# Transpositions of a scan, sums ahead of and behind them, and eight tiles of an FFN put in other places: an encoder block on one core

## The chip, the cores and the metric

The kernel runs on one core of a Trainium2 chip. The metric is the device time of one execution in microseconds (us), as the median of several runs. A profiled execution gives the trace from which the rows below are taken. The engines are PE (TensorE: matmuls, and transpositions as matmuls with an identity), PEld (PE's weight loads, which overlap its matmuls), DVE (VectorE), ACT (ScalarE), POOL (GpSimd) and SP (SyncE, which issues DMAs). Each engine runs its own list of instructions in order and waits, at the head of that list, for what other engines have to deliver.

## The reference

One residual block on x of 512 tokens by 1024 columns, in float32:

```python
x = x + 0.5 * swiglu(rms_norm(x, ffn1_norm), ffn1_w1, ffn1_w3, ffn1_w2)
h = rms_norm(x, mix_norm); p = h @ w_in
y_a = rwkv7_mixer(token_shift(p[..., :SHIFT_COLS]), ...) @ rwkv_proj
y_b = fox_mixer(p[..., SHIFT_COLS:SHIFT_COLS + FOX_COLS], ...) @ fox_proj
x = x + (sigmoid(g_a) * y_a + sigmoid(g_b) * y_b) @ w_out
x = x + 0.5 * swiglu(rms_norm(x, ffn2_norm), ffn2_w1, ffn2_w3, ffn2_w2)
out = rms_norm(x, final_norm)
```

`swiglu(h, w1, w3, w2)` is `(silu(h @ w1) * (h @ w3)) @ w2` with 2816 inner columns. The RWKV-7 mixer is a recurrence over the tokens with one 64 x 64 state for each of 8 heads; the forgetting attention (fox) has 8 heads of 64 with a causal mask and a decay from cumulated logarithms.

## The kernel before

**Layout and precision.** x is kept transposed, as eight tiles of 128 columns by 512 tokens (`xT`). A float32 product is made as three matmuls of rounded halves, `hi*hi + hi*lo + lo*hi` (`mm3`, L142): ACT casts a weight tile into `whi` (L133), DVE subtracts it from the raw tile into `wlo` (L134), and the moving operand is split likewise. SP loads the raw weights through four buffers.

**The stages.** The first FFN, the input projection with the preparation of the recurrence, a scan of 16 steps, the projections of the two mixers, `w_out`, the second FFN and the final norm. In an FFN, 22 inner tiles of 128 rows are made one after the other (`h0` to `h21`, each as `hh` and `hl`). Most are made by a seven-product scheme on halves of 256 tokens (class `Seven`), whose sums of weights lie in the tiles `wsum`, `wtwo` and `wone`. Then come the down products `pd`: eight output tiles, each of 22 x 3 = 66 matmuls of 512 columns, accumulated in the order of the inner tiles, so the 31st to the 42nd of the 66 read `h10` to `h13`. The last output tile of the second FFN is made in two halves of 256 columns, so that the final norm of the first half runs beside the products of the second. Behind each of the first seven output tiles of the second FFN stand four transpositions `ot` of the tile before (L1709).

**Where the tiles lie.** In both FFNs `h10` to `h13` use the eight places of the x tiles, in a pool at the right end of SBUF (`place_h`, L711). As the built program places them, these eight tiles of the first FFN start at byte 288 modulo 512 in every partition, and those of the second at byte 480 modulo 512. The weights `whi`, `wlo`, the tiles `wtwo` and `wone` and all other operands of the products named here start at byte 288 modulo 512.

**The scan.** A step c, of 16, does on PE: some products of the remaining input projections (`some`, matmuls `pq` and `pgt`, which fill the time), the transpositions `turned` of the attention weights, the solve `ups`, the attention's logits `lp`, further products, at some steps a head sum `pq2` (L1161, over two halves `shi` and `slo`; the listings show it as pq), the next state `sps`, the output `yps`, the attention's values, and the read `xps` of the next step. DVE multiplies `sps` by the decay (RD, L1504), and the next read needs both halves of that. Steps at which no attention unit stands behind them (before steps 1, 2, 6 and 10) have no values between `yps` and `xps`. Every second step a group of four transpositions (`vp` of the values, `stage_v`, or `bp` of the keys, `stage_b`) prepares two later steps; ACT copies the result into RD. The PSUM tiles `vp`, `bp`, `ups`, `sps`, `yps`, `xps` and the head sums of the later pairs take three banks in turn, so each waits until the third one before it has been read. A head sum's bank is read by ACT's logarithm (`qrn`, L1165).

**What sets the order.** Instructions that go through `keep` stay in the order of the program; for others a scheduler with its own model of times chooses the order on each engine. `issue_after` puts an instruction behind another in that order.

**Behind the scan.** `fox(m)` is one of eight projections `ppj` (L1553), whose result DVE adds to a gate and multiplies (L1583). Between `fox(0)` and `fox(1)` four centrings `yc` (two matmuls each, L1590) work on the halves of the scan's output, which ACT and DVE split (L170, L171).

**The end.** For each half of the tokens, `final` squares the last tile, sums the squares over the partitions for two token blocks (`os`, L1730: `facc` holds the first seven tiles' squares, `sq` the last tile's), transposes the last tile (`ot`), takes the root on ACT (L1733, L1734), scales four pieces of 512 columns (L1738 on ACT, L1740 on DVE) and stores them (L1741).

## Time and profile before

| | us |
|---|---|
| median of 3 runs | 1140.15 |
| the runs | 1140.03 to 1140.36 |
| the profiled execution, its own time | 1140.51 |
| its span, first to last instruction | 1138.8 |
| PE busy | 1127.8 |
| DVE busy | 830.0 |
| ACT busy | 600.9 |

The mean granted clock of TensorE is 0.999 of full speed. In rows of a timeline the first number is the start in us from the span's start, the second the duration in us, then the engine, the line, the operation, `out<-in` by the program's names without buffer numbers, the shape, the count of instructions merged into the row, and in brackets the idle time of the engine before it with what ended it. A row of a group has the count, then busy us and mean ns of one, or ns as minimum/median/maximum. Matmuls are pipelined, so a matmul's duration is longer than the time from its start to the next one's; the latter is what a stream of them costs. The chain of waits is followed back from the last instruction: each of its rows has a start, a length, the engine and the work.

### The profile page before, as it was taken

Reading aid. Unit: us, or ns where it says so; the run is one execution under the profiler, and the core shown is the slowest. Engines: PE = TensorE matmul, PEld = TensorE weight load, DVE = VectorE, ACT = ScalarE, POOL = GpSimd, SP = SyncE. Lnnn points to the kernel's source line nnn. Section 1 sums busy time; section 2 is a strip of 40 time slices with the busy share of each in tenths; the row PEclk is TensorE's granted clock in tenths of the full one; section 3 lists DMA queues with packets and bytes.
Section 4 is the critical chain, followed back from the end, with each engine's and each line's share of the span. In section 5 each row is a group of like instructions: output and inputs, shape, how many; then the busy total and the mean of one; then the engine's idle time right before and its main releaser. Section 6 shows DMA issues by size and latency. Waiting matters only on the chain.

```text
span 1138.8 us, 19344 instructions
## 1 busy us (share of the span) xinstructions
PE 1127.8 (99%) x7674; PEld 988.1 (87%) x7674; DVE 830.0 (73%) x1301; ACT 600.9 (53%) x1004; POOL 106.8 (9%) x174
## 2 busy tenths in 40 slices
PE   9999999999999999999999999999999999999997
PEld 7899999988887888888777777888999999988887
DVE  6889999953246888777766668879999999943233
ACT  6645665532226754355877757536555566532121
POOL 2000000010111111321000011132000000010000
PEclk9999999999999999999999999999999999999999
DMA  8433333353334333345113236544333333363321
GB/s 260 135 93 109 97 112 111 95 181 115 112 103 124 103 104 103 112 142 139 38 38 100 67 113 200 177 142 126 103 97 108 111 94 112 107 192 91 89 78 74
DMA packets 210729, 131.14 MB, mean 115 GB/s; under 512 B 10415, under 2 KB 200943, under 8 KB 210639
## 3 DMA queue, kind: packets, MB, share of 16 engines
q1 hardware_dynamic: 202078, 108.67, 32.8%
q0 software_dynamic: 6320, 20.45, 5.4%
q8 instruction: 60, 0.98, 0.4%
q10 hardware_dynamic: 2240, 0.79, 0.3%
q14 instruction: 31, 0.25, 0.1%
HBM read 115.02 MB, written 14.88 MB: 114 GB/s over the span
## 4 chain that ended last, share of the span: by engine, by line
PE 96%; DVE 2%; ACT 1%; issue 1%; DVEq 0%; ACTq 0%
PE pd L142 21%; PE za L142 19%; PE zc L142 14%; PE pgt L142 8%; PE pk L142 6%; PE pw L142 4%; PE ppj L1553 4%; PE pb L142 3%; PE pa L142 3%; PE pq L142 3%; PE pv L142 2%; PE pl L142 1%; PE f L309 1%; PE gp L1076 1%; PE lp L1333 1%; PE lp L1347 1%
## 5 line engine op out<-in xcount | busy, mean ns | idle before, releaser
L133 ACT CAST whi<-raw 128x1024 fp32r<-128x1024 f32 (+3 forms) x117 | 113.8, 974 | 238.4 <-PE pd L142 153.7
L134 DVE TENSOR_TENSOR wlo<-raw,whi 128x1024 fp32r<-128x1024 f32 (+3 forms) x117 | 131.9, 1128 | 120.6 <-ACT whi L133 120.3
L142 PE MATMUL pd<-hh,wlo 128*128 128x512 f32 (+1 forms) x332 | 126.5, 381 | 0.0
L142 PE MATMUL pd<-hh,whi 128*128 128x512 f32 (+1 forms) x332 | 126.1, 380 | 0.0
L142 PE MATMUL pd<-hl,whi 128*128 128x512 f32 (+1 forms) x332 | 126.0, 379 | 0.0
L142 PE MATMUL zc<-xh,whi 128*128 128x256 f32 x296 | 83.8, 283 | 0.0
L142 PE MATMUL zc<-xl,whi 128*128 128x256 f32 x296 | 83.8, 283 | 0.0
L142 PE MATMUL zc<-xh,wlo 128*128 128x256 f32 x296 | 83.8, 283 | 0.0
L142 PEld LDWEIGHTS pd<-hl,whi 128*128 128x128 f32 x332 | 62.4, 188 | 12.0
L142 PEld LDWEIGHTS pd<-hh,whi 128*128 128x128 f32 x332 | 62.4, 188 | 11.7
L142 PEld LDWEIGHTS pd<-hh,wlo 128*128 128x128 f32 x332 | 62.4, 188 | 11.6
L142 PEld LDWEIGHTS zc<-xh,whi 128*128 128x128 f32 x296 | 56.8, 192 | 0.0
L142 PEld LDWEIGHTS zc<-xl,whi 128*128 128x128 f32 x296 | 56.8, 192 | 0.0
L142 PEld LDWEIGHTS zc<-xh,wlo 128*128 128x128 f32 x296 | 56.8, 192 | 0.0
L504 ACT CAST wtwo<-wsum 128x1024 fp32r<-128x1024 f32 x37 | 38.8, 1050 | 32.8 <-PE za L142 32.8
L142 PE MATMUL pgt<-xh,whi 128*128 128x512 f32 x128 | 53.0, 414 | 0.0
L507 DVE TENSOR_TENSOR wlo<-raw,whi 128x1024 fp32r<-128x1024 f32 x41 | 50.0, 1219 | 2.7 <-ACT whi L504 2.7
L516 DVE TENSOR_TENSOR wsum<-wsum,raw 128x512 f32<-128x512 f32 x74 | 50.9, 688 | 1.2
L516 DVE TENSOR_TENSOR wsum<-raw 128x512 f32<-128x512 f32 x74 | 50.6, 684 | 0.0
L142 PE MATMUL pgt<-xh,wlo 128*128 128x512 f32 x128 | 50.2, 392 | 0.0
L142 PE MATMUL pgt<-xl,whi 128*128 128x512 f32 x128 | 50.0, 391 | 0.0
L732 POOL DMA_DIRECT2D xP<-xpark x16 | 8.7, 548 | 438.2 <-PE za L142 437.5
(519 smaller groups left out, 3334.0 us busy)
## 6 DMA issues: line engine op xcount, KB each, us to landing
raw<-in_ffn_w_dram SPq DMA_DIRECT2D x118, 512.0 KB
raw<-in_w_in_dram SPq DMA_DIRECT2D x40, 512.0 KB
raw<-in_ffn_w_dram SPq DMA_DIRECT2D x15, 384.0 KB
xP<-xpark POOLq DMA_DIRECT2D x16, 256.0 KB, 4.7
raw<-in_w_out_dram SPq DMA_DIRECT2D x8, 512.0 KB
gsave<-gs SPq DMA_DIRECT2D x9, 256.0 KB
xin<-in_x_dram SPq DMA_DIRECT2D x4, 512.0 KB
xpark<-xT POOLq DMA_DIRECT2D x8, 256.0 KB, 6.3
```

The source lines that it names most:

```text
L133: marks["wide"] = act.copy(hi[:], raw[:])
L134: marks["rest"] = (eng or dve).tensor_tensor(lo[:], raw[:], hi[:].bitcast(F32), op=ALU.subtract)
L142: mm = pe.matmul(ps, w, x_, start=first and n == 0, stop=last and n == 2, skip_group_check=chain)
L309: return keep(pe.matmul(first[w][:], wt, x_[:], start=k == 0 and n == 0, stop=k == KD - 1 and n == 2))
L504: keep(act.copy(dst, src))
L507: keep(dve.tensor_tensor(dst, src, f32(hi), op=ALU.subtract))
L516: keep(dve.tensor_tensor(to, a, b, op=ALU.add))
L732: nc.gpsimd.dma_start(xT[c][:], xpark[c])
L1076: gm = pe.matmul(gps[g][o, c], BK[s, cc], G[p][q][s, cc], start=True, stop=True)
L1333: keep(pe.transpose(s.lps[q][:, k * P:(k + 1) * P], pts[:, q, k * P:(k + 1) * P], ident[:]))
L1347: keep(pe.matmul(av[half(q), j * P:(j + 1) * P], vt[k][:, h * 64:(h + 1) * 64], s.trs[q][:, o:o + P], start=k == 0, stop=k == b))
L1553: keep(pe.matmul(ps[:], a[:, k, :], y[k][b], start=k == 0 and n == 0, stop=k == NP - 1 and n == 2))
```

## The change

**Transpositions of the scan.** A new function `staged(c)` holds the call of `stage_v` or `stage_b`. For steps 1, 2, 6 and 10 it is called at the end of the step before, ahead of the read; for step 4 it is called behind the first group of products of the step; for the others it stays where it was. On PE, at the read before step 2 (yps is the output of step 1, vp the moved transpositions, xps the read, pq the products), before:

```order
L1435 MATMUL xps<-RD_5173,G_3630 32x64
L1435 MATMUL xps<-RD_5173,G_3631 32x64
L1236 MATMUL vp<-ident,V_3792 64x128 x4
L142 MATMUL pq<-xh_3493,whi 128x512
L142 MATMUL pq<-xl_3494,whi 128x512
```

and now:

```order
L1514 MATMUL yps<-G_3630,RD_5172 64x32
L1514 MATMUL yps<-G_3631,RD_5172 64x32
L1236 MATMUL vp<-ident,V_3792 64x128 x4
L1435 MATMUL xps<-RD_5173,G_3624 32x64
L1435 MATMUL xps<-RD_5173,G_3625 32x64
```

The four transpositions, which stood behind the last read, stand ahead of the first one. By the turn of the three banks, `bp` before step 1 now takes the bank of `ups`, `vp` before steps 2 and 6 that of the head sum, and `vp` before step 10 that of `ups`; the reads take that of `sps`. The scheduler also changes the order on ACT here. The logarithm `qrn` of step 1's head sum goes ahead of the last two exponentials instead of between them. On ACT from the copies of `vp` on (qsq and shi are the square and its rounded half for step 2's head sum, tr copies of transposed attention weights, the RD<-ups rows copies of the solve), before:

```order
L1240 COPY RD_5172<-vp 32x4x64 x4
L1155 ACTIVATE qsq<-qk_5077 128x512
L133 CAST whi<-raw 128x1024
L1338 COPY tr<-lp 128x384
L157 CAST shi<-qsq 128x512
L1338 COPY tr<-lp 128x384
L1479 COPY RD_5173<-ups 32x2x64
L1480 COPY RD_5173<-ups 32x2x64
L1479 COPY RD_5173<-ups 32x2x64
L1480 COPY RD_5173<-ups 32x2x64
```

and now:

```order
L1240 COPY RD_5172<-vp 32x4x64 x4
L133 CAST whi<-raw 128x1024
L1155 ACTIVATE qsq<-qk_5077 128x512
L1338 COPY tr<-lp 128x384 x2
L1485 COPY RD_5173<-ups 32x2x64
L1486 COPY RD_5173<-ups 32x2x64
L1485 COPY RD_5173<-ups 32x2x64
L1486 COPY RD_5173<-ups 32x2x64
L157 CAST shi<-qsq 128x512
```

The cast shi moved behind both copies tr and the four copies of the solve, and the square qsq behind the cast of the weights. On DVE the remainder slo of step 2's head sum, which needs shi, goes behind both maxima of the attention instead of between them, and stays ahead of the decay.

**Sums behind the splits.** `fox(m)`'s sum is put behind the last split by `issue_after`. On DVE behind the scan (yklc, yqb and yv are the remainders that the centrings read, G the sum of fox 0, then of fox 1), before:

```order
L171 TENSOR_TENSOR yklc_7094<-V_3792,yklc_7093 128x512
L171 TENSOR_TENSOR yqb_7096<-V_3792,ykb_7095 128x512
L1583 SCALAR_TENSOR_TENSOR G_3624<-G_3624,ppj 128x512
L171 TENSOR_TENSOR yv_7098<-V_3792,yv_7097 128x512
L171 TENSOR_TENSOR yv_7100<-V_3792,yla 128x512
L134 TENSOR_TENSOR wlo<-raw,whi 128x512
```

and now:

```order
L171 TENSOR_TENSOR yklc_7094<-V_3792,yklc_7093 128x512
L171 TENSOR_TENSOR yqb_7096<-V_3792,ykb_7095 128x512
L171 TENSOR_TENSOR yv_7098<-V_3792,yv_7097 128x512
L171 TENSOR_TENSOR yv_7100<-V_3792,yla 128x512
L1594 SCALAR_TENSOR_TENSOR G_3624<-G_3624,ppj 128x512
L134 TENSOR_TENSOR wlo<-raw,whi 128x512
```

The sum of `fox(0)` moved behind the two remainders yv. The scheduler also puts two of ACT's squares of the centrings behind a weight cast instead of around it.

**Places.** A tile `xpad` of 192 bytes is added to the pool of the x tiles, and `fr`, in a pool that lies below it, grows from 176 to 512 bytes. `h10` to `h13` of the second FFN (and the x tiles `xS` before them) move down by 192 bytes, to byte 288 modulo 512. `wsum`, `wtwo`, `wone`, and the final norm's tiles move down by 512 bytes. Nothing else moves.

**The end.** In `final` both `facc` sums go ahead of the transpositions and both `sq` sums behind them, in an order that is kept; the first piece of each half is cut into two of 256 columns, so that five pieces are scaled and stored for four.

```diff
--- before.py
+++ after.py
@@ -168,7 +168,7 @@
 
     def split(dst_hi, dst_lo, src, hi_eng="act"):
         cast = act.copy(dst_hi, src) if hi_eng == "act" else dve.tensor_copy(dst_hi, src)
-        dve.tensor_tensor(dst_lo, src, dst_hi.bitcast(F32), op=ALU.subtract)
+        marks["part"] = dve.tensor_tensor(dst_lo, src, dst_hi.bitcast(F32), op=ALU.subtract)
         return cast
 
 
@@ -1451,6 +1451,10 @@
         def unit(n):
             return units[places.index(n)] if n in places else None
 
+        def staged(c):
+            if c + 2 < NC:
+                (stage_b if c % 2 else stage_v)(c + 2 - c % 2)
+
         parted.extend((0, n, part) for n, part in enumerate(first_parts))
         with tc.issue_after(ahead.ins):
             Xs, taken = read(0)
@@ -1460,11 +1464,13 @@
             u, v = unit(c - 1), unit(c)
             n = some_of[c]
             late_logits = v and c == 12
-            if c + 2 < NC:
-                (stage_b if c % 2 else stage_v)(c + 2 - c % 2)
+            if c not in (1, 2, 4, 6, 10):
+                staged(c)
             with tc.issue_after(taken.ins):
                 flush(100 if c in (1, 12) else 5)
             some(n[0])
+            if c == 4:
+                staged(c)
             if u:
                 u.turned()
             elif c == 0:
@@ -1515,6 +1521,8 @@
                     flush(1.5)
             if u and c + 1 < NC:
                 u.values()
+            if c + 1 in (1, 2, 6, 10):
+                staged(c + 1)
             if c + 1 < NC:
                 Xs, taken = read(c + 1)
             if ends:
@@ -1576,11 +1584,14 @@
             cut = split(*parts[p], vs[p])
         with tc.issue_after(cut.ins):
             logs = act.preload_act_table_set("natural_log_exp_and_others")
+        split_all = marks["part"]
+
         def fox(m):
             g = gslot[m]
             nc.gpsimd.dma_start(g, gsave[KD + m])
             ps = proj(proj_w(m, fox_proj), ybs)
-            dve.scalar_tensor_tensor(g, g, 1.0, ps[:], op0=ALU.add, op1=ALU.mult)
+            with tc.issue_after(split_all.ins):
+                dve.scalar_tensor_tensor(g, g, 1.0, ps[:], op0=ALU.add, op1=ALU.mult)
 
         ycs, sums, roots = [], [], []
 
@@ -1664,6 +1675,7 @@
             late_tanh(m, parted)
         rtp = ctx.enter_context(tc.tile_pool(name="xr2", bufs=1, side="right"))
         xT[:] = [rtp.tile([P, T], F32, name=f"xS{c}", tag=f"xS{c}") for c in range(KD)]
+        rtp.tile([P, 48], F32, name="xpad", tag="xpad")
         for c in range(KD):
             nc.gpsimd.dma_start(xT[c][:], xsave[c])
         ms = []
@@ -1701,7 +1713,7 @@
         fin["O"] = [fp.tile([P, NB, D // 2], F32, name=f"O{i}", tag=f"O{i}") for i in range(2)]
         fin["acc"] = fp.tile([P, T], F32, name="facc", tag="facc")
         fin["sq7"] = fp.tile([P, T], F32, name="sq7", tag="sq7")
-        fin["fr"] = fp.tile([P, 44], F32, name="fr", tag="fr")
+        fin["fr"] = fp.tile([P, P], F32, name="fr", tag="fr")
 
     def tokens(m, b0, nb):
         ps = pr.tile([P, nb, P], F32, tag="b", name="ot")
@@ -1725,20 +1737,24 @@
         hs = slice(b0 * P, (b0 + 2) * P)
         act.activation(fin["sq7"][:, hs], xT[m][:, hs], AF.Square)
         ps = bank("os", pf)
-        for b in (b0, b0 + 1):
-            for t, st in ((fin["acc"], True), (fin["sq7"], False)):
-                pe.matmul(ps[:, b:b + 1], t[:, b * P:(b + 1) * P], ones[:, 0:1], start=st, stop=not st)
+        def add(t, st):
+            for b in (b0, b0 + 1):
+                keep(pe.matmul(ps[:, b:b + 1], t[:, b * P:(b + 1) * P], ones[:, 0:1], start=st and b == b0, stop=not st, skip_group_check=True))
+
+        add(fin["acc"], True)
         tokens(m, b0, 2)
+        add(fin["sq7"], False)
         r = fin["fr"][:, b0:b0 + 2]
         act.activation(r, ps[:, b0:b0 + 2], AF.Ln, bias=epsr[:, 0:1], scale=1.0 / D)
         act.activation(r, r, AF.Exp, scale=-0.5)
-        for b, c, e in ((b0, 0, dve), (b0 + 1, 1, act), (b0, 1, dve), (b0 + 1, 0, dve)):
-            o = fin["O"][c][:, b]
+        w = D // 4
+        for b, c, at, n, e in ((b0, 0, 0, w, dve), (b0 + 1, 1, 0, 2 * w, act), (b0, 0, w, w, dve), (b0, 1, 0, 2 * w, dve), (b0 + 1, 0, 0, 2 * w, dve)):
+            o = fin["O"][c][:, b, at:at + n]
             if e is act:
                 act.activation(o, o, AF.Copy, scale=fin["fr"][:, b:b + 1])
             else:
                 dve.tensor_scalar(o, o, fin["fr"][:, b:b + 1], None, op0=ALU.mult)
-            nc.sync.dma_start(out[0, b * P:(b + 1) * P, c * 512:(c + 1) * 512], o)
+            nc.sync.dma_start(out[0, b * P:(b + 1) * P, c * 512 + at:c * 512 + at + n], o)
 
     ffn(nrm2, ffn2_w1, ffn2_w3, ffn2_w2, almost, final=final,
         seven={"fast": range(2, 22), "from": 1, "to": 22, "sums": (0, 0), "own": 5, "stream": "xS", "places": places, "after": after})
```

## Prediction

> **What bounds the kernel now.** First the busy times of the page, then the waits of PE over the whole span.
>
> ```profile
> PE 1127.8 (99%) x7674; PEld 988.1 (87%) x7674; DVE 830.0 (73%) x1301; ACT 600.9 (53%) x1004; POOL 106.8 (9%) x174
> ```
>
> PE idles 1138.8 - 1127.8 = 11.0 us in all, some of it in the first 16 us, which nothing here touches. A change can save only part of that idle time, or the length of PE's own work. The waits of PE (us in total, times, longest) say how much idle is in reach:
>
> ```profile
> PE xps L1435 <- DVE RD L1504: 1.0, 4, 0.5
> PE ot L1709 <- DVE xP L847: 0.9, 1, 0.9
> PE vp L1236 <- ACT qrn L1165: 0.5, 1, 0.5
> PE yc L1590 <- DVE yv L171: 0.5, 1, 0.5
> ```
>
> Four waits of the scan's reads (xps), one of a transposition (vp), one of the centring (yc), one in the last chain (ot): 2.9 us, and the edits touch each of them.
>
> **1. Transpositions into the waits before steps 1, 2, 6 and 10.** Now they stand behind the read; then, ahead of it, where PE waits for the decay.
>
> ```profile
> 541.34 0.88 DVE L1504 TENSOR_TENSOR RD<-sps,PC 64x256 f32<-64x256 f32 x2
> ...
> 542.27 0.44 PE L1435 MATMUL xps<-RD,G 128*32 128x64 f32 x14 [0.16 <-DVE RD L1504]
> ...
> 543.06 0.48 PE L142 MATMUL pq<-xh,whi 128*128 128x512 f32 x1
> ```
>
> ```profile
> 552.03 0.68 ACT L1165 ACTIVATE qrn<-pq,epsr 128x512 f32<-128x512 f32 x1
> ...
> 552.76 0.47 PE L1435 MATMUL xps<-RD,G 128*32 128x64 f32 x16 [0.51 <-DVE RD L1504]
> ...
> 553.16 0.62 PE L1236 MATMUL vp<-ident,V 128*64 128x128 f32 x4
> ...
> 553.55 0.48 PE L142 MATMUL pq<-xh,whi 128*128 128x512 f32 x1
> ```
>
> ```profile
> 590.63 0.68 ACT L1165 ACTIVATE qrn<-pq,epsr 128x512 f32<-128x512 f32 x1
> ...
> 591.92 0.28 PEld L1435 LDWEIGHTS xps<-RD,G 128*32 128x32 f32 x14 [0.26 <-DVE RD L1504]
> ...
> 592.68 0.48 PE L142 MATMUL pgt<-xh,whi 128*128 128x512 f32 x1
> ```
>
> ```profile
> 629.89 0.44 PE L1435 MATMUL xps<-RD,G 128*32 128x64 f32 x14 [0.16 <-DVE RD L1504]
> ...
> 630.65 0.48 PE L142 MATMUL pgt<-xh,whi 128*128 128x512 f32 x1
> ```
>
> The second half of the decay still ends when it did, and sixteen reads then take 0.40 (552.76 to 553.16), with 0.03 to the next product. So the product starts at 542.70 for 543.06, 553.19 for 553.55, 592.35 for 592.68, 630.32 for 630.65: 0.36 + 0.36 + 0.33 + 0.33 = **1.38 us**. The cover is the wait itself; without it the transpositions cost what they cost now, 0.39 a step (553.16 to 553.55). Queued behind a transposition that waits are the reads, and behind these the step's solve.
>
> It can wait for its PSUM bank. At steps 2 and 6 the bank is the one a head sum leaves, free once ACT's logarithm has read it. At step 2 that ends at 552.03 + 0.68 = 552.71, too late for any gain; but the new order on ACT puts this logarithm before two exponentials, one of 0.47 ahead of it, so it ends about 0.6 sooner. At step 6 it ends at 590.63 + 0.68 = 591.31, which leaves 0.6 to the reads at 591.92 for 0.39 of transpositions. At steps 1 and 10 the bank is long free. I take the full 1.38; at the worst, steps 2 and 6 gain nothing and it is 0.69.
>
> **2. The transposition of step 4, behind a group of products.**
>
> ```profile
> 572.22 0.45 PE L1435 MATMUL xps<-RD,G 128*32 128x64 f32 x16
> ...
> 573.17 0.63 PE L1236 MATMUL vp<-ident,V 128*64 128x128 f32 x4 [0.51 <-ACT qrn L1165]
> ```
>
> Here 0.95 us pass from reads to transposition, where step 2 needs 0.40. The twelve products that go ahead last 2.7 us, so the bank is free when the transposition's turn comes, and the wait goes: **0.5 us**. The copies of its result come later on ACT, behind them those of this step's solve, which the next state needs only after more products; I charge nothing.
>
> **3. What the scan gives back.** ACT's order in step 2 also changes: the cast of the squares (shi) goes behind a copy (tr) and the four of the solved step, and DVE's remainder (slo) waits for it.
>
> ```profile
> 557.34 0.62 ACT L157 CAST shi<-qsq 128x512 fp32r<-128x512 f32 x1
> 557.87 0.48 ACT L1338 COPY tr<-lp 128x384 f32<-128x384 f32 x1
> ...
> 559.50 0.58 ACT L1319 ACTIVATE pts<-lp,mx 128x384 f32<-128x384 f32 x1
> ```
>
> ```profile
> 558.03 0.68 DVE L158 TENSOR_TENSOR slo<-qsq,shi 128x512 fp32r<-128x512 f32 x1
> ```
>
> ```profile
> 560.38 0.40 PE L1161 MATMUL pq<-slo,bonesr 128*128 128x512 f32 x1
> ```
>
> The cast moves back by 559.50 - 557.87 = 1.63, while ACT's queue is about 0.5 ahead by then (0.36 from step 1, some more since step 2's transposition is ready to copy sooner): cast at 558.47 to 559.09, remainder 559.14 to 559.82. PE, 0.72 ahead by then, wants it at 559.66: a new wait of 0.2 us, between 0 and 0.5. The scan nets 1.38 + 0.5 - 0.2 = **1.7 us**.
>
> **4. Remainders ahead of fox 0's sum on DVE.**
>
> ```profile
> 688.25 0.68 DVE L1583 SCALAR_TENSOR_TENSOR G<-G,ppj 128x512 f32<-128x512 f32 x1
> ...
> 688.85 0.68 DVE L171 TENSOR_TENSOR yv<-V,yv 128x512 fp32r<-128x512 f32 x1
> 689.45 0.68 DVE L171 TENSOR_TENSOR yv<-V,yla 128x512 fp32r<-128x512 f32 x1
> 689.58 0.50 PE L1590 MATMUL yc<-yv,center 128*128 128x512 f32 x1 [0.46 <-DVE yv L171]
> ...
> 690.52 0.39 PE L1553 MATMUL ppj<-yh,whi 128*128 128x512 f32 x1
> ```
>
> Each remainder moves up one DVE slot of 0.60. The waiting product starts near 688.98, and the last one, which needs the second remainder (688.85 + 0.68 = 689.53), at 689.58; 0.33 later PE is at the next projection, 689.91 for 690.52: **0.6 us**. The sum ends at 690.13; its bank is wanted again by the projection after next. If its operand were late, nothing is lost: the sum stood ahead of both before.
>
> **5. The second FFN's results 10 to 13.** Modulo 512 bytes the weights lie at byte 288; these eight tiles lie at 480 and move to 288. In the first FFN all lie at 288, so it shows the down products without the offset. From the chain of waits, and from the group of one tile:
>
> ```profile
> 67.97 1.44 PE zc L142 x12
> ...
> 238.43 119.26 PE pd L142 x526
> ...
> 1026.12 15.12 PE pd L142 x66
> ...
> 1041.68 15.09 PE pd L142 x66
> ```
>
> ```profile
> L142 PE MATMUL pd<-hh,whi x4: 276/276/286, 1128.0 to 1129.0; 128*128 128x256 f32 x4
> ```
>
> First FFN: 119.26 / 526 = 0.2267 a product, 14.96 for 66. Second FFN: 15.12 and 15.09, so 0.13 to 0.16 too much for each of seven output tiles, 1.0 at most; part belongs to the transpositions between tiles, which stay. I take **0.6**. The eighth tile runs in halves of 256 columns, and there it goes the other way: 276 ns in the last row, results 10 to 13, where the other 256-column products, all at 288, have 283 (below) at a spacing of 1.44 / 12 = 0.120. Its 24 products lose 24 x 0.007 = 0.15. Net **0.45**, from -0.15 to 0.85.
>
> Rule against row: the Trainium skill, TensorE: Matmul & The Clock Gate, Step-by-step: what each phase is for, says that loading weights does not steal read bandwidth from the running matmul, through two independent read ports. By that rule the place could not matter and this term would be 0. The rows disagree.
>
> **6. The last chain.** PE now sums one token block ahead of the last transposition, and the other behind it; then the facc sums of both stand ahead.
>
> ```profile
> 1131.97 0.36 PE L1730 MATMUL os<-onesr,facc 128*128 128x1 f32 x2
> 1132.19 0.36 PE L1730 MATMUL os<-onesr,sq 128*128 128x1 f32 x2
> ...
> 1133.63 1.80 SPq L1741 DMA_DIRECT2D out_dram<-O  x4
> ```
>
> ```profile
> L1740 DVE TENSOR_SCALAR O<-O,fr 128x512 f32<-128x512 f32 x6 | 2.6, 481 | 1.9 <-ACT fr L1734 1.9
> ```
>
> The facc pair at 1131.97 delays the last one by 0.22 and moves into the 0.9 us wait for xP, which covers it: 0.22. The first store is halved and goes out up to 0.48 / 2 = 0.24 sooner, but there are five issues of 0.45 for four, and pieces of 1 KB a row: between -0.1 and 0.24, I take 0.05, as ACT's half, unmoved, feeds the second store. **0.27**.
>
> **The sum.** 1.7 + 0.6 + 0.45 + 0.27 = 3.0. The profiled execution took 1140.51 (span 1138.8 and 1.7 around it), 0.36 over the median: 1140.51 - 3.0 = 1137.5, and from the median 1140.15 - 3.0 = **1137.1 us**.
>
> **Rivals.** (A) *ACT and DVE set the scan's pace.* What PE saves is handed back at the next head sum or solve, as in part 3. For it: that part; against it: in the waits above no other step of the scan stands. Then 1137.1 + 1.7 = 1138.8. (B) *The place is without effect*, and the second FFN's excess all belongs to its transpositions: 1137.1 + 0.45 = 1137.6; the two FFNs, same order and shapes, speak against it. The rule of the Trainium skill in part 5 would give this case. (C) *Banks late at steps 2 and 6*, so the edit fills only two waits: 1137.1 + 0.7 = 1137.8. (D) *Slower.* The new tile also moves the second FFN's summed weights (wtwo, wone) by 512 bytes. Twenty slots use them in 36 products each, 720, beside operands that stay. If the place counts modulo 1024, each could lose the 6.7 ns of part 5: 4.8 us, 1141.9; it decides once more than 3.0 / 0.0067 = 450 of them are hit. Against it: a product with whi and e00h already has the relation that wtwo and e10h get, and they take the same.
>
> ```profile
> L142 PE MATMUL zc<-e00h,whi 128*128 128x256 f32 x74 | 20.9, 283 | 0.0
> ...
> L142 PE MATMUL za<-e10h,wtwo 128*128 128x256 f32 x148 | 32.8, 284 | 0.1
> ```
>
> **How the numbers follow.** The forecast gets 0.60, A 0.14, B 0.10, C 0.11, D 0.05. Worst terms without D (0.69 + 0.5 - 0.5 + 0.6 - 0.15 + 0.12) leave a gain of 1.3, best ones (1.38 + 0.5 + 0.6 + 0.85 + 0.46) 3.8: 1138.9 and 1136.4 are the range. What can be told from no change is 0.2%, 2.3 us, so faster means under 1137.9: most of the forecast and B, half of C, 0.75 in all; same 0.20 (A, the other half of C); slower 0.05 (D).
>
> **What would show it.** No wait of xps for RD at steps 1, 2, 6, 10 over 0.2, vp not waiting at step 4; a wait of PE for slo in step 2; yc's wait under 0.2; pd at 389 ns throughout in seven tiles and 283 in the eighth; two pairs of os behind the last transposition instead of three. Wrong if ACT's logarithm holds the transposition of step 2, if the spacing of the second FFN's 512-column products stays over 0.2267, or if the summed weights' products leave 283.

## The result, and the profile after

The changed kernel takes 1137.8 us (median of 13 executions, 1137.35 to 1138.53) beside 1140.54 for the kernel before (13 executions, 1140.03 to 1140.93). The ratio is 0.9975, with a 95% interval of 0.9968 to 0.9982: 2.1 to 3.6 us saved. The profiled execution took 1137.8 us with a span of 1136.1, so the spans differ by 2.7.

First the waits of PE over the whole span of the changed kernel.

```profile
PE warm L258 <- DVE ones L84: 1.1, 1, 1.1
PE ot L1721 <- DVE xP L847: 0.7, 1, 0.7
PE f L309 <- DVE xl L294: 0.2, 1, 0.2
PE xtp L284 <- DMA xin<-in_x_dram: 0.2, 1, 0.2
```

All three kinds of wait inside the scan and behind it (xps, vp, yc) are gone from the list, and that of the last chain went from 0.9 to 0.7. No new wait stands in this list, which has PE's matmuls alone; a wait of its weight loads comes up below. Where the time went shows in the starts of the products for which the prediction gave rows, here from PE's timeline of the changed kernel:

```profile
542.79 0.50 PE L142 MATMUL pq<-xh,whi 128*128 128x512 f32 x1
...
552.11 0.63 PE L1236 MATMUL vp<-ident,V 128*64 128x128 f32 x4
552.84 0.45 PE L1435 MATMUL xps<-RD,G 128*32 128x64 f32 x16
553.22 0.50 PE L142 MATMUL pq<-xh,whi 128*128 128x512 f32 x1
...
560.19 0.39 PE L1161 MATMUL pq<-slo,bonesr 128*128 128x512 f32 x1
...
591.63 0.50 PE L142 MATMUL pgt<-xh,whi 128*128 128x512 f32 x1
...
629.33 0.50 PE L142 MATMUL pgt<-xh,whi 128*128 128x512 f32 x1
...
688.61 0.39 PE L1561 MATMUL ppj<-yh,whi 128*128 128x512 f32 x1
```

And from its chain of waits:

```profile
68.04 1.44 PE zc L142 x12
...
1024.11 15.02 PE pd L142 x66
1039.57 14.99 PE pd L142 x66
...
1127.90 0.44 DVE fo L846
...
1129.94 0.27 ACT fr L1748
```

The first row stands 0.07 later than before (68.04 for 67.97): in this execution PE stood a little longer among the first loads. Each start taken from its start before gives the gain up to that place, and the differences of these give each term:

| place | start before | after | gain so far | this place | predicted |
|---|---|---|---|---|---|
| among the first loads | 67.97 | 68.04 | -0.07 | -0.07 | 0 |
| behind the read of step 1 | 543.06 | 542.79 | 0.27 | 0.34 | 0.36 |
| behind the read of step 2 | 553.55 | 553.22 | 0.33 | 0.06 | 0.36 |
| the second head sum product, step 2 | 560.38 | 560.19 | 0.19 | -0.14 | -0.2 |
| steps 4 and 6, up to the read of 6 | 592.68 | 591.63 | 1.05 | 0.86 | 0.83 |
| behind the read of step 10 | 630.65 | 629.33 | 1.32 | 0.27 | 0.33 |
| the second projection behind the scan | 690.52 | 688.61 | 1.91 | 0.59 | 0.6 |
| seven output tiles and the halves of the eighth | 1130.34 | 1127.90 | 2.44 | 0.53 | 0.45 |
| last chain, up to the root | 1132.59 | 1129.94 | 2.65 | 0.21 | 0.22 |
| the end of the span | 1138.8 | 1136.1 | 2.7 | 0.05 | 0.05 |

An output tile of the second FFN costs 15.02 and 14.99 where it cost 15.12 and 15.09, so 0.10 in each of seven. Only one row of the table is far from its prediction: step 2.

### The profile page after: what moved, and what is told of

Read it like the earlier page. It is cut to its first block, busy times and chain, and to the rows that moved or that the text cites. A ratio compares the mean times of both kernels' runs of the same rounds, so it can differ in the third digit from the quotient of the medians.

```text
span 1136.1 us, 19353 instructions
## 1 busy us (share of the span) xinstructions
PE 1127.1 (99%) x7674; PEld 987.3 (87%) x7674; DVE 830.5 (73%) x1303; ACT 600.9 (53%) x1004; POOL 106.7 (9%) x174
## 4 chain that ended last, share of the span: by engine, by line
PE 96%; DVE 1%; ACT 1%; DMA 1%; issue 0%; SPq 0%; DVEq 0%; ACTq 0%
PE pd L142 21%; PE za L142 19%; PE zc L142 14%; PE pgt L142 8%; PE pk L142 6%; PE ppj L1561 4%; PE pw L142 4%; PE pq L142 3%; PE pb L142 3%; PE pa L142 3%; PE pv L142 2%; PE pl L142 1%; PE lp L1347 1%; PE gp L1076 1%; PE lp L1333 1%; PE sps L1508 1%
```

## Step 2: its transpositions put back

```diff
-            if c not in (1, 2, 4, 6, 10):
+            if c not in (1, 4, 6, 10):
                 staged(c)
 ...
-            if c + 1 in (1, 2, 6, 10):
+            if c + 1 in (1, 6, 10):
                 staged(c + 1)
```

> The transpositions of step 2 stand behind its read again, all else as in the changed kernel. If the move was worth what was predicted, 0.36 us are lost at step 2. If DVE sets when the decay before step 2 ends (its queue comes from a weight remainder and two maxima, which didn't move when PE came sooner), the move is all that step 2 gained, and without it the product behind the read starts 0.36 later than in the changed kernel, so the gain of step 1 is lost there: the kernel is 0.3 to 0.4 longer behind step 2. If the bank was late and the move worth only the 0.11 seen in the trace, 0.1.

It took 1137.93 us, with a span of 1136.2. PE at the read of step 2, from its timeline:

```profile
552.40 0.81 PE L1435 MATMUL xps<-RD,G 128*32 128x64 f32 x16 [0.36 <-DVE RD L1510]
...
553.52 0.48 PE L142 MATMUL pq<-xh,whi 128*128 128x512 f32 x1
```

The product starts at 553.52, 0.30 later than in the changed kernel and as late as before the change (553.55). So all of step 1's gain is gone here when step 2 doesn't have its own: the move at step 2 is worth 0.30, but what it saves is the gain that step 1 had already brought, kept instead of lost. That is the second of the three ways expected, up to the read. Up to step 3 half of the 0.30 comes back (560.33 for 560.19), since PE, coming later, waits less there.

Why the gain of step 1 doesn't reach step 2 stands on DVE. Its timeline ahead of that read, in the kernel before:

```profile
551.11 0.78 DVE L1318 TENSOR_REDUCE mx<-lp 128x1 f32<-128x256 f32 x2 [0.33 <-ACT pts L1319]
551.86 0.88 DVE L1504 TENSOR_TENSOR RD<-sps,PC 64x256 f32<-64x256 f32 x2
```

and in the changed kernel:

```profile
551.85 0.85 DVE L1510 TENSOR_TENSOR RD<-sps,PC 64x256 f32<-64x256 f32 x2
```

The decay starts at 551.86 and at 551.85: PE made its products 0.19 sooner (550.94 for 551.13; of step 1's 0.27 the rest was lost along the step), and DVE came to the decay no sooner. Two maxima stand ahead of it, which wait 0.33 for ACT's exponentials, and ahead of these the remainder slo and a remainder of weights (1.2 us) that no change touched.

## Step 2: that remainder elsewhere

Two ways of taking the remainder out of DVE's queue there. The first gives it to GpSimd:

```diff
-                    def ahead_of():
-                        ws.append(split_w(raws.pop(0), KD, P))
+                    def ahead_of(n=n):
+                        ws.append(split_w(raws.pop(0), KD, P, eng=pool if n == 1 else None))
```

> The weight remainder that DVE makes at 548.6 us, ahead of the maxima and of the decay before step 2, is made by GpSimd instead. If DVE's queue sets the end of that decay, the decay ends some 0.3 us sooner than in the changed kernel (552.4 for 552.7), and the product behind the read of step 2 starts 0.25 to 0.3 sooner. If PE's own transpositions or their bank set it, the product stays at 553.2. GpSimd's own time for it is not shown by any row; if it is over 6 us, the products that read it will wait and the gain is lost again.

It took 1140.02 us and doesn't answer the question: GpSimd's subtraction fell beside DVE's work and held it up. From the timelines of GpSimd and of DVE in this run:

```profile
546.63 2.71 POOL L134 TENSOR_TENSOR wlo<-raw,whi 128x1024 fp32r<-128x1024 f32 x1 [9.71 <-ACT whi L133]
```

```profile
547.13 3.47 DVE L1286 TENSOR_TENSOR klc<-qk,kb 64x512 fp32r<-64x512 f32 x2
```

Two subtractions that take DVE 1.41 us in the changed kernel took 3.47; the first began at 547.13, took 2.75 and so ended at 549.88, 0.54 behind the end of GpSimd's (549.34): most of it was waiting for that. PE then waited 1.6 us for the pair. The Trainium skill, SBUF — State Buffer, Who interferes with whom, states that a DVE instruction with two inputs in SBUF contends with a GpSimd instruction that reads SBUF, through a shared port that is an exclusive lock. These rows agree. The second way leaves the remainder on DVE and issues it behind the read of step 2:

```diff
+                        held.append(lambda: dve.tensor_tensor(lo[:], raw[:], hi[:].bitcast(F32), op=ALU.subtract))
 ...
                 Xs, taken = read(c + 1)
+            if c == 1:
+                with tc.issue_after(taken.ins):
+                    held.pop()()
```

> The weight remainder that stands on DVE ahead of the maxima and of the decay before step 2 (1.2 us) is issued behind the read of step 2 instead; its weights are wanted some 3 us later. If DVE's queue holds the decay before step 2 (theory), the decay starts as soon as its products are there and ends 0.2 us sooner than in the changed kernel seen from those products, and the product behind the read of step 2 comes 0.15 to 0.25 sooner; behind step 3 between 0 and 0.25 of that is left, since the remainder now stands ahead of work that the next steps want. If the transpositions or their bank hold the read (rival), the product stays where it is.

It took 1137.8 us, with a span of 1136.1: no change in the whole. From the timelines of DVE and of PE:

```profile
551.78 0.86 DVE L1519 TENSOR_TENSOR RD<-sps,PC 64x256 f32<-64x256 f32 x2 [0.88 <-PE sps L1517]
```

```profile
551.05 0.69 PE L1517 MATMUL sps<-RD,RD 128*64 128x64 f32 x16
...
553.18 0.50 PE L142 MATMUL pq<-xh,whi 128*128 128x512 f32 x1
...
560.17 0.50 PE L1161 MATMUL pq<-slo,bonesr 128*128 128x512 f32 x1 [0.15 <-DVE slo L158]
```

Now DVE stands idle for 0.88 us and takes the decay as soon as PE's products are there. Counted from these products, the read's product comes at 553.18 - 551.05 = 2.13, for 553.22 - 550.94 = 2.28 in the changed kernel (where they start at 550.94): 0.15 sooner, the lower end of what the theory gave. So DVE's queue held step 2, for 0.15 of the missing 0.30. Of the other half, 0.08 was lost before PE came to these products (0.19 left of 0.27). Now the transpositions come as soon as ACT's logarithm has freed their bank (552.24 behind 552.19), and the profile names no other engine that the read behind them waits for. The 0.15 doesn't last: PE, farther ahead, now waits 0.15 for the remainder slo in the same step. That is the wait that the prediction foresaw, 0.2, for the changed kernel, where PE isn't far enough ahead to meet it.

What takes 0.14 back in the changed kernel, between the read of step 2 and its head sum, shows in its timelines of ACT and of PEld:

```profile
556.78 0.86 ACT L1338 COPY tr<-lp 128x384 f32<-128x384 f32 x2
```

```profile
557.32 0.19 PEld L1308 LDWEIGHTS lp<-kb,qa 128*128 128x128 f32 x1 [0.21 <-ACT tr L1338]
```

The second half of the logits waits for the first of ACT's two copies. PE came to the first half 0.28 sooner than before the change (556.66 for 556.94), ACT to its copy only 0.19 sooner (556.78 for 556.97), and the second half follows the first by 0.66 for 0.56: 0.10 of the 0.14. In the run just shown, where ACT made the copy at 555.71, it follows by 0.39 without a wait. The other 0.04 stands in the products just behind the read; what takes it is not shown.

## The place of the tiles: a sweep

The eight tiles of `h10` to `h13`, each 64 bytes farther along than the one before (`fr` goes back to its 176 bytes, so that the weights stay at byte 288):

```diff
-        xT[:] = [rtp.tile([P, T], F32, name=f"xS{c}", tag=f"xS{c}") for c in range(KD)]
-        rtp.tile([P, 48], F32, name="xpad", tag="xpad")
+        for c in range(KD):
+            xT[c] = rtp.tile([P, T], F32, name=f"xS{c}", tag=f"xS{c}")
+            rtp.tile([P, 16], F32, name=f"xpad{c}", tag=f"xpad{c}")
```

> The eight tiles of h10 to h13 in the second FFN lie each 64 bytes farther than the one before, modulo 512: seen from the weights' byte 288, h10 (hi, lo) at +192, +256, h11 at +320, +384, h12 at +448, 0, h13 at +64, +128. Theory 1: a 512-column product is spaced 0.2267 us where its operand lies at the weights' byte, and 0.2333 everywhere else, so only the lo half of h12 is at 0.2267, and in the last tile of 256 columns it alone is at 0.120, the others at 0.1133. Theory 2: only a part of the circle costs more, around +192 or +256; the small offsets 64, 128, 448 stay at 0.2267. Theory 3: it isn't the relation but that operands which change from tile to tile share nothing; then no product changes against the changed kernel. The whole is 0.4 to 0.9 us longer than the changed kernel by theory 1, 0 to 0.5 by theory 2, 0 by theory 3.

It took 1137.57 us in one execution, which stood 0.55 ahead of the changed kernel's profile already at the first slots. An output tile shows the cost, in the chain of waits:

```profile
1023.58 15.08 PE pd L142 x66
```

0.06 more than the 15.02 of the changed kernel, and the others stand the same way, 0.4 for the seven, the lower end of what the first theory gave. But the single products don't follow it: they are spaced 0.224 to 0.239 without a clean value for any place, and the tile at the weights' own byte (the lo half of h12) is no exception among them, nor at 0.120 in the last tile. The cost hangs on the place; it is not a price per product that its own place sets.

## The products of 256 columns: weights moved, tiles moved

In the kernel before, the tiles at +192 bytes made the 512-column products slower and the 256-column ones faster. A slot here is one inner tile made by the seven-product scheme, of 7 x 12 = 84 products; the 37 slots of both FFNs have 3108 products of 256 columns. First, the summed weights of the second FFN 192 bytes lower:

```diff
-        fin["fr"] = fp.tile([P, P], F32, name="fr", tag="fr")
+        fin["fr"] = fp.tile([P, P + 48], F32, name="fr", tag="fr")
```

> The summed weights wtwo and wone of the second FFN lie 192 bytes lower (byte 96 modulo 512), so that their operands lie at +192 seen from them. They are read in 36 products of 256 columns in each of 20 slots, 720 in all. Theory 1 (a 256-column product is faster with the operand at +192, 0.1133 for 0.120 us, whichever of the two was moved): 720 x 0.0067 = 4.8 us less than the changed kernel, 1133.0, and durations of 276 ns for 283. Rival (it was a property of the last tile, or of where the operand lies and not of the relation): no change, 1137.8. A third way: the sums' products are bound by something else there and gain only where two of them follow each other, some 24 of 36: 3.2 us.

1136.17 us (five executions, 1135.77 to 1137.14), 0.9962 of the kernel before (0.9947 to 0.9976); in the trace the slots of the second FFN, from the first product to the last, are 1.7 us shorter than in the changed kernel (200.59 for 202.25). The products with wtwo and wone are spaced 0.1177, not 0.1133. The direction is right and the size is not: a third of the first theory, less than the third way.

Then everything together to byte 0, each relation kept:

```diff
+    cp.tile([P, 56], F32, name="cpad", tag="cpad")
     xp = ctx.enter_context(tc.tile_pool(name="xp", bufs=1))
 ...
+    ctx.enter_context(tc.tile_pool(name="top", bufs=1, side="right")).tile([P, 72], F32, name="tpad", tag="tpad")
     vtp = fctx.enter_context(tc.tile_pool(name="vtp", bufs=1, side="right"))
```

> All tiles of the tensor work are moved together, from byte 288 modulo 512 to byte 0, so every relation between an operand and its weights stays. If only the relation counts: the spacings stay at 0.2267 and 0.120 and the time at 1137.8. If the byte itself counts too (the run with the sums moved gave 0.1177 where the tiles moved before had given 0.1133, at the same relation): spacings change, by the steps seen so far by 0.0067 up or down: with some 3100 products of 256 columns and 3300 of 512, 20 us each way.

1137.21 us in one execution. All spacings are those of the changed kernel (its lead is 0.4 us at the first slots and 0.5 at the last down product). Where operand and weights lie at the same byte, which byte that is doesn't count.

Then the operands: sixteen tiles of summed inputs at eight places.

```diff
                 hi, lo = [s.hp.tile([P, T], F32R, name=f"e{i}{n}{t}", tag=tags[2 * i + j]) for j, t in enumerate("hl")]
+                s.hp.tile([P, 16], F32, name=f"epad{i}{n}", tag=f"epad{i}{n}")
```

> The sixteen tiles of the summed inputs, e00 to e31, lie 64 bytes farther modulo 512 from pair to pair (hi and lo of a pair at the same place): from the weights' byte e00 at 0, e10 at +64, e20 at +128, e30 at +192, e01 at +256, e11 at +320, e21 at +384, e31 at +448. Each pair is read by six products of 256 columns in a row. If the relation decides, each six have a spacing of their own: 0.120 for e00, 0.1133 for e30 (the place that h10 to h13 had before), between or equal for the others. If products in other places only fall out of a common rhythm, all but e00 take something between, 0.117 to 0.119, whatever the place. The whole: 37 slots x 42 products x up to 0.0067 = up to 10 us less than the changed kernel by the first, 3 us by the second.

1134.82 us in one execution. From the groups of the tiles za and zc, with duration as minimum/median/maximum:

```profile
L142 PE MATMUL za<-e10h,wtwo x148: 276/280/393, 70.5 to 992.9; 128*128 128x256 f32 x148
...
L142 PE MATMUL za<-e20h,wtwo x148: 280/282/285, 73.3 to 996.2; 128*128 128x256 f32 x148
...
L142 PE MATMUL za<-e31h,wone x148: 276/276/277, 76.9 to 999.7; 128*128 128x256 f32 x148
```

```profile
L142 PE MATMUL zc<-e01h,whi x74: 283/283/284, 72.6 to 994.8; 128*128 128x256 f32 x74
```

The place decides here, and it counts modulo 256: e01 at +256 has 283 ns, as all had; e10 at +64 (and e11 at +320) 279 to 280, spaced 0.1177; e20 at +128 282, irregular around 0.119; e30 at +192 and e31 at +448 come to 276, spaced 0.1133 from the fifth of the twelve products on. Behind these the products of other operands, at the weights' byte, are also short for a while: twelve take 1.42 us for 1.44.

A finer sweep moved the operands of the first FFN to the places between (+32, +96, +160, +224), and in the second FFN the weights:

```diff
+                first = s.nrm is nrm
+                if first and i == 0:
+                    s.hp.tile([P, 24], F32, name=f"epad{n}", tag=f"epad{n}")
                 hi, lo = [s.hp.tile([P, T], F32R, ...
+                if first:
+                    s.hp.tile([P, (48, 32, 16, 8)[i]], F32, name=f"epad{i}{n}", tag=f"epad{i}{n}")
 ...
         wsum, wtwo = fp.tile(...), fp.tile(...)
+        fp.tile([P, 16], F32, name="wpad", tag="wpad")
 ...
-        fin["fr"] = fp.tile([P, P], F32, name="fr", tag="fr")
+        fin["fr"] = fp.tile([P, P - 48], F32, name="fr", tag="fr")
```

> First FFN: the weights stay at byte 288 modulo 512, the tiles of the summed inputs lie, seen from there and modulo 256, at +96 (e00, e01), +32 (e10, e11), +160 (e20, e21), +224 (e30, e31). Second FFN: the tiles of the summed inputs stay, and the weights wtwo lie at +128, wone at +192. If the spacing is a property of the relation alone, modulo 256, the second FFN has what the sweep of the operands had for -128 and -192: about 0.1187 with wtwo and 0.1177 with wone. If the weights' own byte counts too, wone can be anything from 0.107 to 0.120. For the places +32, +96, +160 and +224 of the operands no row stands; by the neighbours 0.1133 to 0.120 each, and +224, next to +192, the lowest. The whole is 1 to 5 us below the changed kernel.

1135.29 us in one execution. The four places between give 0.118 to 0.120 and no clean rhythm. The second FFN is the find. From the group of the tile za there, the products with wone at +192:

```profile
L142 PE MATMUL za<-e30h,wone x76: 276/276/276, 809.8 to 989.4; 128*128 128x256 f32 x76
```

With the weights at +192 the spacing is 0.1133 from the first product of the twelve on, where the operand at +192 had needed four products to get there. With wtwo at +128 it is irregular, about 0.1187. By the relation alone 0.1177 was expected for wone: modulo 256, its operands lie 64 bytes behind it, as e10 and e11 lay behind wtwo in the first sweep. So the relation alone doesn't set the spacing.

## Versions built on this

First the operands: all sixteen tiles at +192 in both FFNs.

```diff
+            s.hp.tile([P, 48], F32, name=f"epad{n}", tag=f"epad{n}")
             for i, e in enumerate((e1, e2, e3, e4)):
 ...
                 s.E[i].append((hi, lo))
+            s.hp.tile([P, 80], F32, name=f"epod{n}", tag=f"epod{n}")
```

> All sixteen tiles of the summed inputs lie 192 bytes behind the weights' byte modulo 512, in both FFNs; all else as in the changed kernel. In the sweep twelve products in a row with such a tile took 1.379 us for 1.440, and the twelve behind them, with tiles at the weights' byte, 1.42. Here 36 stand in a row and then 12 alone in each of 37 slots: 48 x 0.0067 = 0.32 less, minus some 0.02 at the start of each row, plus 0.02 behind it. By the relation alone: 37 x 0.32 = 11.8 us less than the changed kernel, 1126 us. If the gain needs the products of other operands between, as the sweep's whole would allow (0.125 a slot): 4.6 us less, 1133.

1127.42 us (four executions, 1126.67 to 1127.91), 0.9878 of the kernel before (0.9862 to 0.9895). One slot of the second FFN in its chain of waits:

```profile
897.42 1.38 PE za L142 x12
898.80 1.36 PE zc L142 x12
900.16 1.36 PE za L142 x12
901.52 1.42 PE zc L142 x12
902.94 2.80 PE za L142 x24
```

Where each twelve took 1.44, the three groups with a moved operand take 1.38, 1.36 and 1.36, the next 1.42, the next twenty-four (twelve moved, twelve not) 2.80. The whole gains 10.4 us of the 11.8 worked out. In the trace the slots themselves are 11.6 shorter (5.2 and 6.4 in the two FFNs); the profiled execution came to its first slot 0.75 later than that of the changed kernel and spent 0.2 more in the down products.

Then the weights instead, which enter the rhythm at once: whi, wlo, wtwo and wone of all slots and whi and wlo of the last output tile at +192, by tiles that are longer by 192 and 320 bytes and are used from their start or from behind. No instruction changes its place in any engine's order.

```diff
+    def w_pair(kt, n, far):
+        got, i = [], turns[0] % 2
+        turns[0] += 1
+        for name, pad, at in (("whi", 48, (0, 48)), ("wlo", 80, (80, 0))):
+            t = wp.tile([P, KD * P + pad], F32R, tag=f"{name}{i}", name=name, bufs=1)
+            got.append(t[:, at[far]:at[far] + kt * n].rearrange("p (k n) -> p k n", n=n))
+        return got
 ...
-                    new["a"] = s.pair()
+                    new["a"] = s.pair(True)
 ...
-                    new["c"] = s.pair()
+                    new["c"] = s.pair(True)
 ...
+        hp.tile([P, 48], F32, name="wpad", tag="wpad")
         wtwo, wone = hp.tile(...), hp.tile(...)
 ...
-        fin["fr"] = fp.tile([P, P], F32, name="fr", tag="fr")
+        fin["fr"] = fp.tile([P, P - 48], F32, name="fr", tag="fr")
```

> The operands stay at byte 288 modulo 512; the weights of all seven products of every slot (whi, wlo, wtwo, wone), and whi and wlo of the last output tile, lie 192 bytes behind that, in both FFNs. The instructions and their order on every engine are those of the changed kernel. From the sweep (wone at +192: 0.1133 from the first product on): 37 x 84 x 0.0067 = 20.7 us less in the slots and 96 x 0.0067 = 0.6 in the last tile: 1137.8 - 21.3 = 1116.5 us, with all of za and zc at 0.1133. If whi and wlo do not act as wone did (rival; no run had them there), only the 24 products of E2 and E3 and the 12 of E4 gain: 37 x 36 x 0.0067 = 8.9, 1129 us. One output tile of the second FFN, the fourth, has its weights there too, with 512 columns: 0.2333 a product as the moved operand had, 0.44 us longer in all; or 0.220, if the lock that 0.2267 has is worth 0.0067 less by this side, 0.44 shorter.

1124.36 us in the median of four executions, but these took 1123.57, 1123.69, 1125.03 and 1130.79: neither of the two sums. The chain of waits of the profiled one (1123.57), in the first FFN, at the start of the second, and later in it:

```profile
99.13 1.41 PE za L151 x12
...
797.78 1.41 PE za L151 x12
799.19 1.18 PE zc L151 x11
800.37 0.28 ACT fa L513
800.70 1.63 PE za L151 x12
802.33 1.36 PE zc L151 x12
...
900.25 1.36 PE zc L151 x12
```

The same products with the same bytes have two spacings: 1.41 for twelve, 0.1178 from start to start, in the whole first FFN, and 0.1133 in the second from a wait of PE at 800.4 on. So the bytes alone don't set the spacing; it is a rhythm that goes on until something disturbs it. In the sweep wone had come behind products at 0.120 and gone to 0.1133; here the slots come behind 512-column products and go to 0.1178. What ran just before isn't the whole of it either: e10 in the first sweep and the summed weights in the first run came behind products at 0.120 too and had 0.1177. The fourth output tile, with 512 columns and its weights at +192, takes 0.229 a product: a loss, so that these stay at the operands' byte.

If what ran before decides it here, it is enough to lead in with some products at 0.120 (`kind` is "S" when the slot before is one of the scheme, so all slots but the first of each FFN have these weights moved):

```diff
-                    new["a"] = s.pair(True)
+                    new["a"] = s.pair(kind == "S")
```

> As the run before (all weights of the slots 192 bytes behind their operands), but the first 24 products of each FFN's first such slot have weights and operand at the same byte, and the fourth output tile has its weights where the others have them. In the run before, the products went on at 0.1178 wherever they came behind products of 512 columns or a wait (all of the first FFN, and the second up to 804 us), and at 0.1133 where they came behind 256-column products at 0.120. Theory: the spacing is a state that lasts, taken over from what ran before, and 24 products at 0.120 lead into the state at 0.1133. Then all slots behind the first steps run at 0.1133, the executions agree among themselves again (they spread over 7 us), and the time is 1137.8 - 3108 x 0.0067 - 0.4 + 0.3, about 1117 us. Rival: the state is taken at random or from something else, such as the place of the tiles in the first FFN; then the first FFN stays at 0.1178 and the time at 1123 to 1131.

1124.25 us in the median of five executions: four took 1124.21 to 1125.80, one, which has no trace, 1118.00. The chain of waits of a profiled one (1124.21), in the first FFN and in the second:

```profile
86.98 1.36 PE zc L151 x12
...
792.86 1.44 PE zc L151 x12
794.33 1.68 PE za L151 x12
...
902.01 1.41 PE zc L151 x12
```

The first FFN runs at 0.1133 from the lead on to its end, as the theory said. In the second PE waits for the same copy as before, at 794 us, just where the lead ends, and goes on at 0.1178; in the run before, the same wait had brought it from 0.1178 to 0.1133. So a wait can throw the rhythm either way, as far as these two traces tell; no run put a wait in by itself. The cure is to lead in again, at slots 4 and 12:

```diff
-                    new["a"] = s.pair(kind == "S")
+                    new["a"] = s.pair(kind == "S" and j + 1 not in (4, 12))
```

> As the run before, but the first 24 products with weights and operand at the same byte come again at slots 4 and 12 of each FFN. In the run before, the first FFN held 0.1133 from its first slot to its last, and the second fell to 0.1178 behind a wait of 0.2 us of PE for a copy of ACT in its first slot and held that to the end; four of five executions took 1124 to 1126 us, one 1118.0. If the state is led in by such products and lasts until PE waits: the second FFN runs at 0.1178 up to slot 4 and at 0.1133 behind it, the three more groups cost 3 x 24 x 0.0067 = 0.5 us, and all executions take about 1118. If the state falls at random, without a wait, the executions spread over 1118 to 1126 again.

**1118.42 us** (five executions, 1117.92 to 1118.86), 0.9804 of the kernel before (0.9791 to 0.9818): 22 us less than it, 19 less than the changed kernel. The second FFN in its chain of waits:

```profile
808.67 1.41 PE zc L151 x12
810.08 2.85 PE za L151 x24
812.93 1.44 PE zc L151 x12
814.37 1.36 PE za L151 x12
815.73 1.36 PE zc L151 x12
```

At 1.41 up to slot 4, at 1.44 in its lead, at 1.36 behind it. The first FFN in a window of the changed kernel and the same window of this one (length, then for each engine busy time and instructions, the granted clock, the DMA's share and its GB/s):

```profile
66.00:230.00 164.00, 164.00 (x1367) 163.92 (x1366) 153.22 (x227) 97.97 (x147) 0.00 (x0) 1.00 0.37 106
```

```profile
66.00:230.00 164.00, 164.00 (x1438) 163.69 (x1437) 157.43 (x236) 98.90 (x152) 4.36 (x8) 1.00 0.40 118
```

PE is busy all the time in both, with the clock at 1.00, and does 1438 products where it did 1367. The busy time says nothing of the difference; the count does.

## Why the prediction was right, and where it was not

1137.1 was forecast from the median of three executions, and 1137.8 is the median; from the profiled execution 1137.5, and 1137.8 was profiled. Of the 0.7 between 1137.1 and 1137.8, 0.4 is the base: the kernel before has a median of 1140.54 over 13 executions, and had 1140.15 over three. The rest is the gain: 3.0 was worked out, and 2.7 came, between the medians and between the spans.

- **Part 1, transpositions into the waits.** Right at steps 1, 6 and 10 (0.34, 0.31, 0.27, for 0.36, 0.33, 0.33). Rival C fell, but not by much: ACT's logarithm did hold the transposition of step 2, which starts at 552.11, just behind the logarithm's end at 552.05 and some 0.1 later than PE could have; it was still done before the decay ended at 552.70, so this cost nothing. At step 6 the logarithm ended at 590.56, just ahead of the transposition at 590.61. Wrong in the sum at step 2, and that is the term that was mis-sized: 0.36 by the prediction, 0.06 measured. The start itself was right (553.19 forecast, 553.22 measured). But "553.19 for 553.55" and "542.70 for 543.06" were added as if the second were counted from a step that came 0.36 sooner, while the sentence under them said that the decay ends when it did. Both can't hold: a decay that ends when it did takes the earlier gain back. The runs showed which: undone, the move at step 2 costs 0.30, and DVE's queue, not PE, sets when that decay starts (the read's product comes 0.15 sooner when the remainder is taken out of the queue). At steps 6 and 10 DVE comes with PE, and there the gains do add up.
- **Part 2, step 4.** Right: 0.50 (PE's lead grows from 0.22 at the step's read to 0.72 at the transposed attention weights, 575.67 for 576.39), and with step 6 0.86 for 0.83.
- **Part 3, what the scan gives back.** 0.14 for 0.2, but not by the wait that was named: PE, only 0.33 ahead, doesn't wait for slo in the changed kernel. That wait stands in the run in which PE is farther ahead. What takes most of the 0.14 (0.10) stands ahead of it: the logits of step 2 wait for ACT's copy tr, which came only 0.19 sooner. So the size was near by luck: two errors met, PE taken as 0.72 ahead where it was 0.33, and this wait left out.
- **Part 4, remainders ahead of fox 0's sum.** Right, 0.59 for 0.6.
- **Part 5, results 10 to 13.** 0.53 for 0.45: 0.10 for each of seven tiles (0.086 in the prediction), less what the eighth lost. In the third output tile, for one, the twelve products that read `h10` to `h13` were spaced 0.2333 before and are at 0.2267 now, 0.08 in all; the other 0.02 stood in the five products behind them. Rival B is refuted: the place has an effect, in the prediction's two rows and by 19 us in the last run above, and the measurement decides. The Trainium skill (TensorE: Matmul & The Clock Gate, Step-by-step: what each phase is for) says that loading weights takes no read bandwidth from the running matmul, and by the prediction's reading of it the place could not matter. Whether it is read bandwidth that the two share, no run shows. The mechanism behind the term was too simple all the same: in the sweep the place wasn't a price per product.
- **Part 6, the last chain.** Right: 0.21 and 0.05.
- **Rival A**, that ACT and DVE hand it all back, holds at one step of five, step 2, and there for both: DVE's queue keeps the decay, ACT's copy the logits. **Rival D**, the summed weights losing 6.7 ns each, is refuted: their products keep 283 ns.

## What to carry to other kernels

Before two savings at waits for the same engine are added, look at whether what ends the second wait moves with the first saving; a time of day at which something ends isn't a length. Where a stage is bound by a stream of matmuls, take the spacing from start to start, by length and by the place of operand and weights, since PE's busy time reads 99% whether twelve products take 1.44 us or 1.36. Then try the place of the weights against that of the operands, by tiles a little longer: here it was worth seven times the whole change, with no instruction moved.

## What the runs showed of the hardware that was not expected

- 256-column products of float32 operands run in one of several lasting rhythms. With weights and operand at the same byte modulo 256 it is 0.1200, whichever byte that is (0 or 288 modulo 512). With the two 64 bytes apart, either way, it is 0.1133 or 0.1177 to 0.1178. At other places it is irregular, 0.118 to 0.120. (Weights 192 bytes behind the operand are, modulo 256, 64 in front of it.) Products of 512 columns have their best, 0.2267, at the same byte, 0.229 with the weights and 0.2333 with the operand at +192.
- Both ways of lying apart have shown both rhythms. Operands 192 bytes behind their weights had 0.1133 when the operands were moved, and 0.1177 when the summed weights were moved instead, though both came behind products at 0.120. With the weights 192 bytes behind, all slots took 0.1178 behind 512-column products, and 0.1133 behind a lead of products at 0.120 that no wait of PE followed. A wait of 0.2 to 0.3 us came once with a change from 0.1178 to 0.1133, and twice with 0.1178 where a lead had gone before. A rhythm then lasted for over a thousand products.
- Why the bytes matter, and what else decides between the two rhythms, no run shows: the trace has the starts of weight loads and matmuls, and not the reads.
- A subtraction of 0.69 us on DVE took 2.75 beside one of 2.71 on GpSimd.
